# Copying half rows in 1 KB descriptors instead of 16 KB ones, with another spacing of the rows over the DMA engines

## Chip, cores and metric

The kernel runs on one core of one Trainium2 chip. The metric is the device time of that core in microseconds, lower is better. Before the change it is 822.16 us (median; 5 runs, 821.42 to 822.79).

## What is computed

```python
def setup_inputs():
    return {"x": np.random.randn(8192, 8192).astype(np.float32)}

def reference(x):
    return np.fft.ifftshift(x)      # both axes: roll by 4096 rows and 4096 columns
```

Output row r is input row (r + 4096) mod 8192 with its two halves exchanged. Nothing is calculated: 268.44 MB are read from HBM and 268.44 MB written, in contiguous pieces of at most half a row (16 KB).

## The kernel before

Two issuing engines, SyncE and ScalarE, copy from HBM to HBM. One takes the left halves of the output rows, the other the right halves. Each has a queue, and each DMA is shared out over sixteen DMA engines (the traces show 16 landings for each). A descriptor is one contiguous piece of a DMA; the trace records it as a packet. HBM is the memory that holds input and output.

```python
ENGINES = 16
STEP = 4
PER = 16
...
    dims = [[STEP * C, ENGINES], [STEP * ENGINES * C, PER], [1, hc]]
    block = STEP * ENGINES * PER
    ...
        queues = [
            (nc.sync, 0, nc.alloc_semaphore("left")),
            (nc.scalar, hc, nc.alloc_semaphore("right")),
        ]
        n = 0
        for base in range(0, R, block):
            for c in range(STEP):
                row = base + c
                src_row = (row + hr) % R
                for eng, h, sem in queues:
                    eng.dma_start(
                        out=bass.AP(out.tensor, out.offset + row * C + h, dims),
                        in_=bass.AP(x.tensor, x.offset + src_row * C + hc - h, dims),
                    ).then_inc(sem, 16)
                n += 1
        for eng, _, sem in queues:
            eng.wait_ge(sem, 16 * n)
```

A DMA is 16 engines x 16 rows x 16 KB = 4 MB. The engines are 4 rows (128 KB) apart and an engine's rows 64 apart; 32 such DMAs go to each queue.

## Time and profile before

The lines are in the prediction below. What matters of them:

| | before, first profile |
|---|---|
| share of the span that the DMA engines are occupied | 49.8% + 49.6% |
| rate in the steady stage, each way | 333 to 334 GB/s |
| a 16 KB packet, by the packet records: minimum / mean | 608 / 784.5 ns |
| wait for queue space: a DMA issue, minimum / median | 0.64 / 23.5 us |

The engines always have a packet in hand, but it takes 173 ns longer on average than at the engines' own pace. The prediction calls these 173 ns the hold-up.

The time of that first profiled execution was 810.7 us, below every untroubled run of this kernel measured later (818.8 to 825.0 on several chips). A second profile, shown under the result, is the better measure.

### The profile page before, as it was taken

What the parts mean: (1) busy time and instruction counts of PE and PEld (TensorE: products, weight loads), DVE (VectorE), ACT (ScalarE), POOL (GpSimd) and SP (SyncE); (2) the same over time, 40 slices, a digit from 0 to 9 for tenths busy, and PEclk for the clock granted to TensorE, in tenths of its full rate; (3) what the DMA queues carried; (4) which work ended last, traced back from release to release, by engine and by line L of the source; (5) the groups of instructions that cost most, each with busy time, mean ns of one, the idle gap of its engine ahead of it and who ended that gap; (6) DMA issues with size and microseconds to landing.
All of it is one profiled execution on the core that took longest, in us unless ns stands there. A gap on an engine that the chain in (4) does not pass through costs nothing. (4 is left out here: it accounts for less than half of the span.)

```text
span 808.9 us, 115 instructions
## 1 busy us (share of the span) xinstructions
POOL 0.2 (0%) x4
## 2 busy tenths in 40 slices
POOL 0000000000000000000000000000000000000000
DMA  8999999999999999999999999999999999999998
GB/s 301 333 336 332 338 330 334 335 332 332 335 335 332 331 335 334 335 329 337 331 335 333 331 333 332 341 334 332 332 335 335 332 338 331 333 331 335 334 331 297
DMA packets 17408, 268.44 MB, mean 332 GB/s; under 512 B 1024, under 2 KB 1024, under 8 KB 1024
## 3 DMA queue, kind: packets, MB, share of 16 engines
q1 hardware_dynamic: 8704, 134.22, 49.8%
q10 hardware_dynamic: 8704, 134.22, 49.6%
HBM read 268.44 MB, written 268.44 MB: 664 GB/s over the span
## 5 line engine op out<-in xcount | busy, mean ns | idle before, releaser
L60 POOL MEMSET const-uint8-127<- 128x1 uint8 x1 | 0.1, 103 | 0.0
L60 POOL MEMSET const-bfloat16-1.0<- 128x1 bf16 x1 | 0.1, 102 | 0.0
L60 POOL MEMSET const-float32-0.0<- 128x1 f32 x1 | 0.1, 99 | 0.2 <-issue 0.2
L60 POOL MEMSET const-float32-1.0<- 128x1 f32 x1 | 0.1, 99 | 0.0
## 6 DMA issues: line engine op xcount, KB each, us to landing
out_dram<-in_x_dram ACTq DMA_DIRECT2D x32, 4096.0 KB, 154.8
out_dram<-in_x_dram SPq DMA_DIRECT2D x32, 4096.0 KB, 154.9
```

Of the source, the lines that this page charges most:

```text
L60: nc = _bacc.Bacc("TRN2", target_bir_lowering=False, num_devices=1)
```

## The change

The intent, as its code shows: let the two queues alternate in small pieces, so that both halves of a row are under way at nearly the same time, and space the rows differently. With 1 KB pieces the pattern gains a dimension, and the engine and row dimensions are merged into one of 64 rows. Here and in the prediction it is taken that engine e then gets four consecutive ones of these, 8 rows apart, so that the engines are 32 rows (1 MB) apart. The traces hold no addresses, so this is not shown. A DMA moves 1 MB, and each queue gets 128.

```diff
-STEP = 4
-PER = 16
+STEP = 8
+PER = 4
...
-    dims = [[STEP * C, ENGINES], [STEP * ENGINES * C, PER], [1, hc]]
+    dims = [[STEP * C, ENGINES * PER], [1, hc]]
...
                         in_=bass.AP(x.tensor, x.offset + src_row * C + hc - h, dims),
+                        max_dma_last_dim=1024,
                     ).then_inc(sem, 16)
```

## The prediction

> **What bounds the kernel now.** I read the page from the top: engines, the 40 slices, the DMA queues, the chain, the DMA issues. Then stretches of the span, the waits of the issuing engine, the issuing line, and last the single packet records of the trace.
>
> ```profile
> span 808.9 us, 115 instructions
> ...
> POOL 0.2 (0%) x4
> ...
> DMA packets 17408, 268.44 MB, mean 332 GB/s; under 512 B 1024, under 2 KB 1024, under 8 KB 1024
> ...
> q1 hardware_dynamic: 8704, 134.22, 49.8%
> q10 hardware_dynamic: 8704, 134.22, 49.6%
> HBM read 268.44 MB, written 268.44 MB: 664 GB/s over the span
> ...
> out_dram<-in_x_dram ACTq DMA_DIRECT2D x32, 4096.0 KB, 154.8
> out_dram<-in_x_dram SPq DMA_DIRECT2D x32, 4096.0 KB, 154.9
> ```
>
> No engine computes: four tiny memsets are all the busy time, so the chain of computing work is empty and says nothing. The two queues occupy the sixteen DMA engines for 49.8% + 49.6% = 99.4% of the span. There are 17408 - 1024 = 16384 data packets of 16 KB (a half row is 4096 x 4 B = 16384 B) and 1024 tiny ones, one per engine and DMA (64 DMAs x 16). Every byte is read from HBM and written to HBM, hence 332 GB/s each way and 664 GB/s in sum.
>
> ```profile
> 20.00:100.00 80.00, 0.00 (x0) 1.00 1.00 334
> 100.00:400.00 300.00, 0.00 (x0) 1.00 1.00 333
> 400.00:700.00 300.00, 0.00 (x0) 1.00 1.00 334
> ```
>
> ```profile
> SPq L28 <- DMA out_dram<-in_x_dram: 131.9, 1, 131.9
> ```
>
> ```profile
> L39 SPq DMA_DIRECT2D out_dram<-in_x_dram x32: 637/23450/58192, 1.0 to 652.3; - x32
> ```
>
> These are three answers: stretches (start:end, length, POOL busy, clock, DMA share, GB/s), the wait of the issuing queue, and the issuing line. The stretches show one flat stage at DMA share 1.00 and 333 to 334 GB/s. The only wait of SyncE that matters is the last one, 131.9 us for the landings. The issuing line (minimum/median/maximum ns) takes 637 ns when there is room and 23450 ns at the median: the issuers wait for queue space, so issuing isn't the limit.
>
> The engines are always occupied, but not always at full speed. In the packet records the 16 KB packets have a floor of 608 to 611 ns (a quarter of them are below 612), a median of 758, a 95th percentile of 1093 and a mean of 784.5. Check: 1024 data packets per engine x 784.5 ns = 803.3 us, 99.3% of 808.9. So of each packet 611 ns is the engine's own pace and 173 ns is held up by something. Is that private bad luck or a shared limit? I averaged the packets begun in each 20 us: if delays were independent, the averages would scatter by 8.3 ns; they scatter by 4.0, and neighbours are negatively correlated. What one engine gains another loses. I read this as a **shared limit**: HBM with its mix of reads and writes, at 664 GB/s.
>
> **What the Trainium skill says.** "HBM Reference", section Specifications (TRN2), gives about 716 GB/s per domain. The trace's 664 GB/s is 93% of that, if both tensors lie in one domain, which the trace doesn't tell. It agrees with the shared limit and caps the gain: 536.9 MB / 716 GB/s = 750 us (an estimate from that page).
> "DMA: Bandwidth & Descriptors", section "Why small descriptors are slow (HBM only)", states about 3 cycles of fixed cost per packet inside the engine. The trace agrees: an 8 KB packet (instruction fetch) has a minimum of 307 ns and a 16 KB packet 611, so (611 - 307) / 8 = 38 ns per KB and 611 - 16 x 38 = 3 ns fixed.
> "Advanced Engine Details and Errata", section Clock Domains, gives 42 to 43 ns for an unobstructed 1 KiB descriptor. My fit gives 38 + 3 = 41 ns; no 1 KB packet is in the trace before.
> The first page again, section "Why a DMA increments its semaphore by 16 and not by 1": the slowest dimension is divided over the engines. [...]In the trace before, each DMA has 16 landings, which agrees.
>
> **The change part by part.** The instruction order shows 32 DMAs of 16x16x4096 elements on each queue becoming 128 of 64x16x256, and nothing else.
> (1) Data descriptors: 16384 become 268.44 MB / 1024 B = 262144, 16384 per engine. Engine floor: 16384 x 41 ns = 672 us (with 42.5 ns: 696 us), against 1024 x 611 ns = 626 us before. That is 46 to 70 us more of the engines' own time. But the steady stage has 803 - 626 = 177 us of held-up time per engine. Under a shared limit the new cost lies inside this: it is hidden. Cost 0; I allow 4 us for less overlap near saturation.
> (2) Semaphore packets: 256 DMAs x 16 / 16 = 256 per engine instead of 64, at the 7 ns the small packets take: 192 x 7 ns = 1.3 us, hidden likewise.
> (3) Issuing: the fastest issue takes 631 ns for 16 x 17 = 272 descriptors, at most 2.3 ns each. A new DMA has 16 x 65 = 1040, so at most 1040 / 272 x 631 ns = 2.4 us; 128 per queue make 309 us, in parallel on two queues. Even if one generator served both it is 618 us, under 809. Not the bound.
> (4) Depth: a DMA now lands in 154.9 us, with one per queue finishing each 808.9 / 32 = 25.3 us: 6.1 are in flight, about 104 descriptors per engine and queue. The same count at 1 KB is 104 KB instead of 1.7 MB. Over two queues at 21 GB/s per engine this is still some 10 us ahead, 13 times a 16 KB packet's time. Enough, I expect.
> (5) Tail: the last 4 MB DMAs land unevenly (DMA share 0.91 in the last 29 us, so 2.6 us lost); with 1 MB DMAs perhaps 1 us comes back.
> (6) Memory order: a 16 KB run of one half, then one of the other, becomes 1 KB of each alternately; engines go from 4 to 32 rows apart and an engine's rows from 64 to 8. This changes which addresses meet at the memory. It can move the shared limit itself, either way, and no row of the profile prices it.
> Sum of what I can price: 808.9 + 4 - 1 = 812 us of span. The runs' median is 822.16 - 808.9 = 13.3 us above the profiled span. Total 825; I say **824 us**.
>
> **The rivals.**
> Rival A, the hold-up stays per byte: 173 / 16 = 10.8 ns per KB is added to 41 ns. 16384 x 51.8 ns = 849 us, plus 5.6 us not covered by packets before, plus 13.3: **868 us**, 5.6% slower. For it: a quarter of the packets run at the floor, odd for a pool that is always full; short packets may also stall more often. Against: the averages scatter half as much as independent delays would.
> Rival B, the finer interleaving helps the memory: both halves of a row are touched within tens of ns instead of a packet apart, and long bursts no longer block the other queue. Its end is 750 + 5.6 + 13.3 = 769 us; half of the way is **795**, 3% faster. For it: only 626 / 809 = 77% of the engines' time is work at their own pace, so there is something to win, and the new engine floor (672 to 696) leaves room. Against: 93% of the stated peak, with reads and writes mixed, is already high.
> Rival C, many small transactions: too few bytes in flight per engine and queue, or the generator waits for the slowest ring and starves others. Gaps between packets would then appear. An allowance of 5 to 15% more gives **860 to 940**. For it: the first packets of the run take 1054 to 1439 ns against 611, so some 500 ns of latency must be covered, 12 descriptors of 1 KB in flight per engine instead of one of 16 KB. Against: point 4.
>
> **Range and chances.** The main path gives 824. B pulls down to 795 and hardly under 780; A and C pull up to 868 and beyond. I take 785 to 890 as the range. Faster by over 2% means below 806 and needs the memory at 677 GB/s or more, 95% of the stated peak: 0.30. Within 2%: 0.35. Slower, above 839, by A or C: 0.35.
>
> **What would show it right or wrong.** Right: DMA share stays at 1.00 with about 332 GB/s, 1 KB packets with a floor near 41 ns and a mean near 49 (803 us / 16384), some 266,000 packets in all, issue times long at the median (queue full), no gap between packets. A is right if the mean is near 52 ns at share 1.00. B is right if the rate goes beyond 340 GB/s and the mean falls to 48 ns or less. C is right if the share falls below 0.95 or issues never wait. Wrong altogether: a 1 KB floor far above 43 ns, which makes the engines the bound, or issues that take more than 6 us each while the DMA share drops, which makes generation the bound.

## The result

The changed kernel takes **844.32 us** (median of 5, 843.55 to 845.06) against 822.16: ratio 1.0271, 95% interval 1.0257 to 1.0285, so it is slower. Ratios here are the mean time of one kernel's fast runs over that of the other's of the same rounds, so not quite the ratio of the medians that are quoted. They also put aside that sessions and chips differ: the median of the kernel before was 819.3 to 824.6 us, and 821.7 and 824.6 in two sessions on chip 3 alone.

First the kernel before, profiled again: the span and the HBM line of its page, then the stretches.

```profile
span 820.6 us, 115 instructions
...
HBM read 268.44 MB, written 268.44 MB: 654 GB/s over the span
```

```profile
20.00:100.00 80.00, 0.00 (x0) 1.00 1.00 328
100.00:400.00 300.00, 0.00 (x0) 1.00 1.00 328
400.00:700.00 300.00, 0.00 (x0) 1.00 1.00 330
```

Its time was 822.4 us with this span of 820.6, so only 1.8 us lie outside the span, not the 13.3 of the prediction. The usual rate is 328 to 330 GB/s, and the usual mean of a 16 KB packet 795.1 ns. The first profile had caught a quicker execution. Whether that was another chip isn't recorded.

Now the changed kernel: its page, its stretches, the wait of the issuing queue and the issuing line.

```profile
span 842.4 us, 307 instructions
...
DMA packets 266242, 268.47 MB, mean 319 GB/s; under 512 B 4096, under 2 KB 266240, under 8 KB 266240
...
q10 hardware_dynamic: 133120, 134.23, 51.3%
q1 hardware_dynamic: 133120, 134.23, 51.2%
...
HBM read 268.44 MB, written 268.44 MB: 637 GB/s over the span
...
out_dram<-in_x_dram ACTq DMA_DIRECT2D x128, 1024.0 KB, 24.2
out_dram<-in_x_dram SPq DMA_DIRECT2D x128, 1024.0 KB, 24.3
```

```profile
20.00:100.00 80.00, 0.00 (x0) 1.00 1.03 319
100.00:400.00 300.00, 0.00 (x0) 1.00 1.03 320
400.00:700.00 300.00, 0.00 (x0) 1.00 1.03 320
```

```profile
SPq L28 <- DMA out_dram<-in_x_dram: 15.4, 1, 15.4
```

```profile
L39 SPq DMA_DIRECT2D out_dram<-in_x_dram x128: 732/6418/9520, 1.0 to 819.6; - x128
```

The loss is spread evenly: every stretch runs at 319 to 320 GB/s instead of 328 to 330. No stage is new, and issuing isn't the limit: the issuers still wait for queue space (6418 ns at the median, 732 when there is room). The share now exceeds 1.00. A queue's share is the sum of its packets' durations, and 51.3% + 51.2% can only come from packets of one engine that overlap in the records. So the recorded duration of a small packet is longer than the pace at which packets follow each other, and durations must not be multiplied by counts here. The records give 46 ns for 95% of the 1 KB packets, a mean of 52.55, and 260 ns on average for the 3% of them that exceed 86 ns. Many packets run at the floor and few are held up long.

### The profile page after: what moved, and what is told of

Same layout as the page of the kernel before. It is cut to its first block, busy times and chain, and to the rows that moved or that the text cites. A ratio compares the mean times of both kernels' runs of the same rounds, so it can differ in the third digit from the quotient of the medians.

```text
span 842.4 us, 307 instructions
## 1 busy us (share of the span) xinstructions
POOL 0.2 (0%) x4
## 3 DMA queue, kind: packets, MB, share of 16 engines
q10 hardware_dynamic: 133120, 134.23, 51.3%
q1 hardware_dynamic: 133120, 134.23, 51.2%
## 6 DMA issues: line engine op xcount, KB each, us to landing
out_dram<-in_x_dram ACTq DMA_DIRECT2D x128, 1024.0 KB, 24.2
```

## The experiments

The theories, as they stood after the two profiles:

- **T1**: the fixed cost of more packets takes engine time, and the hold-up absorbs only part of it.
- **T2**: the new row layout disturbs the memory.
- **T3**: smaller DMAs leave too little in the queues.
- **T4**: 1 KB pieces disturb the memory, not the engine.

### The kernel before again

> The kernel before once more, for its profile beside its time. The first profile showed a span of 808.9 us, while its untroubled runs took 822. If the span is some 820 now, 822 is the usual time and the first profile fell in a quicker execution or on another chip; if it is 809 with a time of 822, 13 us lie outside the span, as the prediction took it.

822.41 us, span 820.6: the first alternative.

### The new layout with 16 KB descriptors

```diff
 # from the changed kernel
-                        max_dma_last_dim=1024,
```

> The new row layout and the 1 MB DMAs, with 16 KB descriptors as before. Theory T1 (the 1 KB packets cost the engines 46 ns against 38 ns per KB, and the memory's hold-up absorbs only a part): this run goes back to the kernel before, 818 to 826 us. Rival T2 (the addresses: engines 32 rows apart, an engine's rows 8 apart, disturb the memory): it stays at 838 to 850 us. Rival T3 (the smaller DMAs leave too little in the queues): also near 844.

823.38 us, ratio 1.0014 (0.9997 to 1.0031): the same as before. With 16 KB descriptors the layout and 1 MB DMAs cost 0.3% at most; T2 and T3, as they were stated, fall.

### The old layout with 1 KB descriptors

```diff
 # from the kernel before: a DMA for each p, 16 rows each
-    dims = [[STEP * C, ENGINES], [STEP * ENGINES * C, PER], [1, hc]]
+    dims = [[STEP * C, ENGINES], [1, hc]]
...
+                for p in range(PER):
+                    row = base + c + STEP * ENGINES * p
...
+                            max_dma_last_dim=1024,
```

> The old row layout, in the old order, with 1 KB descriptors (in DMAs of 16 rows[...]). T1: 840 to 850 us, as the changed kernel. T2: 818 to 826 us, as before. T3: slower than the changed kernel, as its DMAs are a quarter as large: 850 and more.

837.27 us, ratio 1.0189 (1.0173 to 1.0204). The 1 KB descriptors alone bring 15.5 of the 22 us, below T1's 840 to 850 and T3's 850 and more. Some 7 us of the changed kernel are missing, though its layout cost nothing with 16 KB: descriptor size and layout (or DMA size) work together.

### 4 KB descriptors in the new layout

```diff
-                        max_dma_last_dim=1024,
+                        max_dma_last_dim=4096,
```

> The changed kernel with descriptors of 4 KB. T1: the fixed 8 ns are paid once in 4 KB, a floor of 161 ns or 40.2 ns per KB instead of 46; the time is near the kernel before, 820 to 830 us. T2: the layout stays, so 844. If interleaving the halves finely were good or bad for the memory as such, the time lies off the line between 16 KB and 1 KB.

828.59 us, ratio 1.0082 (1.0067 to 1.0097): between the two, as T1 said.

### Eight engines: what a descriptor costs the engine itself

Only eight of the sixteen engines copy, in DMAs of 8 rows, once with 16 KB and once with 1 KB descriptors.

```diff
 # from the old layout with 1 KB in DMAs of 16 rows
-ENGINES = 16
-STEP = 4
+ENGINES = 8
+STEP = 8
...
-                            max_dma_last_dim=1024,
+                            max_dma_last_dim=16384,      # the 16 KB run only
```

> The whole copy on eight of the sixteen DMA engines, 16 KB descriptors (8 rows a DMA). At their own pace of 611 ns a packet plus 9 ns for the semaphore packet, 2048 packets an engine give 1270 us, 211 GB/s each way, far below the 327 that sixteen reach. If the hold-up comes from a limit that the engines share, nearly all packets now take 611 ns and the span is 1270 to 1300 us. If it is private to each engine (rival A of the prediction), packets still average 795 ns and the span is some 1640 us.

> The same on eight engines with 1 KB descriptors. 32768 packets an engine at 46 ns, and 2048 semaphore packets at 9 ns: 1526 us. T1 (the cost is the engine's fixed 8 ns per packet, hidden only while the shared limit binds): 1530 to 1560 us, 20% above the 16 KB run of eight engines, where sixteen engines show 2 to 3%. If the 1 KB packets cost at the memory instead, and not at the engine: within 3% of the 16 KB run of eight engines.

1287.67 and 1409.52 us (one run each, so without an interval). The same stretch of each, 16 KB first:

```profile
400.00:700.00 300.00, 0.00 (x0) 1.00 0.51 213
```

```profile
400.00:700.00 300.00, 0.00 (x0) 1.00 0.54 192
```

With eight engines the hold-up is gone: 16 KB packets average 612.9 ns instead of 795. The limit that holds packets up is shared by the engines, and rival A's private delays fall. The descriptor cost, bare, is 9.5% by the times; these include a tail of the 16 KB run (26 GB/s in its last 26 us), so the steady rates are better. From the rates, eight engines at 213 GB/s need 16384 x 8 / 213 = 615 ns for 16 KB, and at 192 GB/s 1024 x 8 / 192 = 42.7 ns for 1 KB, semaphore packets included. Fifteen more packets thus cost 16 x 42.7 - 615 = 68 ns, **4.5 ns each**, not the 8 that I had read from the 46 ns records; hence 1409 and not the expected 1530. The packet records agree: 1 KB packets that follow each other start 42 or 43 ns apart. With sixteen engines that is 15360 x 4.5 = **69 us** more engine time for each engine, of which 22 show in the changed kernel and 15.5 in the old layout.

### Engine time that touches no HBM

After each DMA of the control a second one moves eight pieces of 128 B per engine from SBUF to SBUF, that is, between tiles in the core's own memory. The control itself is the kernel before in DMAs of 16 rows.

```diff
+                        p0, f0 = 16 * (m % 8), 256 * (m // 8)
+                        eng.dma_start(
+                            out=dst[p0 : p0 + 16, f0 : f0 + 256],
+                            in_=src[p0 : p0 + 16, :],
+                            max_dma_last_dim=128,
+                        ).then_inc(sem, 16)
+                        m += 1
```

> The control of the next run: old row layout, 16 KB descriptors, in DMAs of 16 rows (512 a queue instead of 32). 820 to 826 us; more would be the price of small DMAs, and would explain a part of the changed kernel by T3.

> The control plus a DMA after each of its DMAs that moves 8 pieces of 128 B per engine from SBUF to SBUF: engine time that touches no HBM, 1024 x (8 x about 12 + 9) ns = some 108 us per engine, near the 123 us that 15360 more packets at 8 ns give in the changed kernel. T1 (engine time is absorbed by the hold-up but for a fifth): 16 to 24 us above the control. Rival T4 (engine time is absorbed wholly, and the 1 KB pieces spoil the order of accesses at the memory): 0 to 4 us above the control.

The control took 823.91 us (ratio 0.9994), so small DMAs cost nothing with 16 KB. The padded kernel took 835.70 (ratio 1.0136): 11.8 us more, between the two theories. What a pad DMA costs an engine where nothing absorbs it was to be measured on eight engines, from the same edit (8 partitions a pad, semaphores of its own; one run):

> The pieces of 128 B from SBUF to SBUF beside the copy on eight engines with 16 KB descriptors, where the engines and not the memory set the pace: it measures what one pad DMA costs an engine. 2048 of them; by the packets' records (8 x 13.1 + 9 = 114 ns) they would add 233 us to the 1288 us; if packets overlap by some 4 ns, as the 1 KB packets on eight engines do, 160 to 180 us, that is 80 to 88 ns each, and the sixteen engines of the padded run then carried 80 to 90 us of it each, of which 12 showed.

1537.38 against 1287.67 us: 249.7 us for 2048 pads, 122 ns each. But this isn't what a pad costs an engine, because in this run issuing sets the pace. The issuing lines of SyncE, copies first:

```profile
L48 SPq DMA_DIRECT2D out_dram<-in_x_dram x1024: 676/677/860, 1.4 to 1528.8; - x171
L54 SPq DMA_DIRECT2D pad_dst<-pad_src x1024: 712/723/781, 2.3 to 1529.5; - x171
```

Both medians lie close to their minimum, so the issuers never wait for room: a queue issues a copy and a pad in 1.49 us, and 1024 such pairs make the run. The 122 ns are only an upper bound. The packet records of the same run show the pace: pieces of 128 B that follow each other start 9 or 10 ns apart (each recorded with 13 ns), and a pad with its semaphore packet takes an engine some 81 ns, as was expected. The sixteen engines of the padded kernel therefore carried about 1024 x 81 ns = 83 us each, and 11.8 showed: **some six sevenths of plain engine time is absorbed**. (The padded DMAs land in 13.9 us against 59 in the control, so shorter queues may have a part in the 11.8.) If the 69 us of the 1 KB descriptors were absorbed alike, they would show as 9.8 us (an estimate from these runs). T1 is a part of the answer, but alone it is too small.

The packet records also show where the rest appears. In the second profile of the kernel before, an engine has 1024 x 615 ns of pace and 1024 x (795.1 - 611) ns of hold-up, 630 + 189 = 819 of 820.6 us. In the changed kernel it has 16384 x 42.7 and 16384 x (52.55 - 46) ns, 700 + 107 = 807 of 842.4 us. The recorded hold-up shrank by more than the engine time grew, but some 35 us are left in which an engine has no packet in the records. These gaps can be counted: between 100 and 700 us fewer than fifteen packets are under way in 10% of the time, against 0.4% in the kernel before and 0.1% in the padded kernel. On eight engines with 1 KB fewer than eight are under way in less than 0.1%. So 1 KB packets on sixteen engines bring gaps that plain engine time doesn't bring. Whether these are queues that run dry or hold-up that falls between the records of short packets stays open.

### 512 B descriptors

```diff
-                        max_dma_last_dim=1024,
+                        max_dma_last_dim=512,
```

> The changed kernel with descriptors of 512 B. On eight engines 1 KB took 42.2 ns of pace and 16 KB 38.0 per KB, so about 4.3 ns are fixed; 512 B then takes 23.3 ns, and 32768 of them 764 us, still under 822. T1 says that what shows grows faster than linearly as the engine time nears the memory's limit: 870 to 900 us. If what shows is a fixed price at the memory per descriptor (1 KB showed 21 us for 15360 more per engine), 512 B shows 43: 865 us. If the engine were the only bound, no less than 764 us, and the time would not rise at all.

858.57 us, ratio 1.0478 (1.0452 to 1.0505), 39 us above before. T1's 870 to 900, with what shows growing faster than linearly, is missed; the fixed price's 865 is nearer. Shown per added descriptor and engine are 6.9 us / 3072 = 2.2 ns at 4 KB, 22.2 / 15360 = 1.4 at 1 KB and 38.9 / 31744 = 1.2 at 512 B. It is nearer to a price per descriptor, one that falls, than to engines that run out of slack: in the records 512 B packets that follow each other start 23 or 24 ns apart, 770 us for 32768, far below 858.57.

### The new layout with 1 KB in DMAs of 16 rows

```diff
 # from the changed kernel; the same order of rows for each engine
-    dims = [[STEP * C, ENGINES * PER], [1, hc]]
+    dims = [[STEP * PER * C, ENGINES], [1, hc]]
...
+                for p in range(PER):
+                    row = base + c + STEP * p
```

> The changed kernel's row layout, order of rows and 1 KB descriptors, in DMAs of 16 rows (512 a queue) instead of 64. It parts the two things in which the changed kernel (844 us) differs from the old layout with 1 KB in DMAs of 16 rows (837 us). If the row layout makes the 7 us: 842 to 847 (ratio about 1.026). If the size of the DMAs makes it: 835 to 840 (ratio about 1.019).

856.46 us (853.58 to 861.96), ratio 1.0459 (1.0412 to 1.0506). It meets neither number: it is slower than the changed kernel (1.0271). So with 1 KB both seem to matter. At equal DMA size the new layout is 2.7 points worse than the old one (1.0459 against 1.0189; the runs were on two chips, each against the kernel before on its own). And in the new layout DMAs a quarter as large cost 1.9 points more, where with 16 KB they cost nothing. (The changed kernel's chip isn't recorded, and that both runs give an engine the same rows is taken from the code, as said under the change.)

The issue lines of this run show how short its queues are:

```profile
out_dram<-in_x_dram ACTq DMA_DIRECT2D x512, 256.0 KB, 13.3
out_dram<-in_x_dram SPq DMA_DIRECT2D x512, 256.0 KB, 13.3
```

From issue to landing 13.3 us pass, against 24.2 in the changed kernel and 155 in the kernel before. The old layout with 1 KB lands as fast (13.4 and 13.6) and is quicker, so short queues by themselves aren't the cause.

### Engines 31 rows apart

If engines that keep step meet at the memory because their distance is a round number of bytes, an odd distance should help.

```diff
 # from the run before
-    dims = [[STEP * PER * C, ENGINES], [1, hc]]
+    dims = [[pitch * C, ENGINES], [1, hc]]    # pitch 31; 8 for the last 128 rows of each half
```

> As the run with the new layout in DMAs of 16 rows and 1 KB descriptors (856 us, ratio 1.046), but with the engines 31 rows apart instead of 32 (the last 128 rows of each half: 8 apart). With 1 KB the row layout came to matter (837 against 856 us at equal DMA size), which with 16 KB it did not (ratio 1.001). Theory T5: engines that work at the same place of their rows at the same time meet at the memory, the more so the rounder the distance is in address (32 rows are 1 MB): with 31 rows the ratio falls to 1.02 or less, 840 us. Rival T6: it is the distance as such (engines spread over 16 MB instead of 2 MB), or the order of one engine's own rows: the ratio stays at 1.04 to 1.05. Whatever comes, 1 KB stays slower than the kernel before if the price of the pieces themselves remains (ratio above 1.01).

844.72 us, ratio 1.0302 (1.0288 to 1.0316). One row less between the engines takes back 1.6 of the 2.7 points at the same DMA size. So a part of the layout's price seems to hang on the exact distance, as T5 says, though that engines meet at the memory is not shown. It doesn't reach T5's 1.02, and the rest stays open (the distance as such, or the order of an engine's rows, which are 8 apart here and 64 apart in the old layout). The 31-row and the 32-row run were on two chips, and the 32-row one scatters over 1%. No version beats the kernel before.

## Why the prediction was right or wrong

The 844 us lie in the range of 785 to 890, and "slower" had 0.35. But the point of 824 and its path, "hidden, within 2%", did not come true. Slower had its chance from rivals A and C, and what the runs show is neither of them as stated, so that the range holds is owed to its width. By its steps:

- **Bound.** Right: a shared limit. The kernel before shows packets of 795 ns on sixteen engines and 612.9 on eight. The sign read from the trace (averages that scatter by half of what independent delays give) had pointed the right way; the negative correlation of neighbours adds nothing, as redone it is -0.1 over 39 averages. That the limit lies in HBM itself is not shown by any run.
- **Step (1), size of the engine cost.** Right: 46 to 70 us were worked out, 69 measured, with the 42.7 ns pace near the 42 to 43 ns of the Trainium skill ("Advanced Engine Details and Errata", section Clock Domains). The fit to the trace, 41 ns with 3 ns fixed, was low against 4.5. The 46 ns of the records would have misled.
- **Step (1), "it is hidden. Cost 0; I allow 4 us".** This is the step that failed. Plain engine time is indeed absorbed for six sevenths, so that an estimated 9.8 us of the 69 would show. But 1 KB descriptors showed 15.5 us in the old layout and 22 in the new one. The recorded hold-up did give way (189 to 107 us an engine), but some 35 us without a packet came up, where the prediction expected "no gap between packets".
- **Step (6), memory order.** It was named and left at zero. Its distances of 32 and 8 rows rest on the sharing of rows that the traces don't show; the section that the prediction cites last, on the semaphore (it is in "DMA: Bandwidth & Descriptors"), tells how many engines share a DMA, not which rows each gets. With the old layout about 6 us (15.5 - 9.8) are neither absorbed nor plain engine time, so something in how 1 KB pieces meet the queues or the memory costs them; which of these was not separated. The rest, some 7 us, comes with the layout and DMA size at 1 KB. With 16 KB the same layout costs nothing, and with 1 KB it costs 22 us or so at equal DMA size.
- **Steps (2) to (4).** Right in that issuing didn't bind: 6.4 us at the median is waiting for room, at share 1.03. An issue with room took at least 681 ns for 1040 descriptors, against the ceiling of 2.4 us. The depth of (4) was put at some 10 us; 24.2 us passed from issue to landing. A semaphore packet of (2) takes 9 ns in the records, not 7.
- **The sum.** The 808.9 us were a quick execution and the 13.3 us outside the span don't exist (1.8 do). The two errors cancelled, since 822 was the right start.
- **Rival A** (868 us, the hold-up stays at 10.8 ns per KB). Its sign, a mean near 52 ns, seemed to appear (52.55), but the durations overlap. In paces, the changed kernel needs 842.4 us / 16384 = 51.4 ns per KB, 8.7 above the bare 42.7; the second profile of before gives 820.6 us / 16384 = 50.1, and 50.1 - 615 / 16 = 11.7. Gaps counted in, the hold-up shrank from 11.7 to 8.7 ns; full hiding needed 7.4.
- **Rival B**, finer interleaving helps: refuted as a gain on balance. The rate fell, and finer still (512 B) it fell further.
- **Rival C**, gaps: half met. Its signs (a share below 0.95, issues that never wait) didn't come, but overlapping records lift the share, and the count of packets shows gaps all the same. The issuers mostly waited for room (6.4 us at the median). What opened the gaps is not known; engines that run unequally behind one queue are a rival that no run tested.

## What to carry to other kernels

Where all DMA engines wait on a limit that they share, added engine time was mostly free here (11.8 of some 83 us showed), but smaller descriptors are not the same as added engine time: measure them apart, with padding that touches no HBM. Running on half of the engines shows in one go whether a packet's duration is the engine's own or the shared limit's, and what a descriptor really costs, as long as the issue times show that issuing doesn't set the pace. Where records overlap, a share above 1.00 doesn't rule out gaps: count the packets under way. Large descriptors also make the kernel forgiving: with 16 KB no change of row spacing or DMA size that was tried moved the time by 0.2%, with 1 KB they mattered by up to 2.7%.

## What the Trainium skill lacked or had wrong

- "DMA: Bandwidth & Descriptors", section "Why small descriptors are slow (HBM only)": it gives a fixed cost of about 3 cycles per packet, in cycles only; eight engines show 4.5 ns. It lacks what remains of it from HBM to HBM on sixteen engines, where a shared limit holds packets up: 1 KB costs 1.9 to 4.6% of the time by layout and DMA size, and 512 B 4.8%.
- The same page, section "Latency and other measured facts", row on the HBM row pitch: it tells of pitches from 512 KiB up with 16 KiB pieces. Here engines 128 KB or 1 MB apart were alike with 16 KB pieces (ratio 1.0014), but with 1 KB pieces, in DMAs of 16 rows, 1 MB gave 1.0459, 31 rows (992 KB) 1.0302 and 128 KB 1.0189. Its explanation by streams in lock-step is neither shown nor refuted by this.
- "HBM Reference", section Specifications (TRN2): it gives a rate for one core that streams alone, but none for one core that copies from HBM to HBM; the row just named has such copies, at 214 GB/s per direction at most. Measured: 327 GB/s each way, 654 in sum.
- "Perfetto Trace Analysis", section "DMA Engine Tracks": it says that slices show actual busy time. In the packet records of these traces small packets overlap: 46 ns recorded at a pace of 42.7, and shares up to 1.09 (512 B).
